# Bank readings ahead of the weights' steps in a decoder block on one core, with a mean and roots of norms in other operations

## The chip, the core and the metric

The kernel is one launch on one core of a Trainium2 chip. TensorE (PE) multiplies and writes into banks of PSUM, VectorE (DVE) and ScalarE (ACT) read and empty these banks and do the elementwise work, GpSimd (POOL) and SyncE (SP) issue DMAs. Each engine works through its own list of instructions in order, and waits at an instruction until what it reads is written and what it writes is free. The metric is the time of one execution on the device in microseconds (us), as a median over runs.

## The reference

A hybrid decoder block, in f32, over 512 tokens of width 1024:

```python
h = h + 0.5 * swiglu(rms_norm(h, g_ffn1), w_ffn1_gate, w_ffn1_up, w_ffn1_down)   # inner width 2816
u = rms_norm(h, g_mix)
z = u @ w_in                          # conv GLU | q | k | v | merge gates
y_conv = conformer_conv(a_glu, ...)   # GLU, 31-tap depthwise conv, LayerNorm, silu, @ w_conv_out
y_attn = o.reshape(b, s, ATTN_OUT_W) @ w_attn_out      # dilated windowed attention, 3 groups
h = h + (g_a * y_conv + g_b * y_attn) @ w_mix_out      # the mixers' output
h = h + 0.5 * swiglu(rms_norm(h, g_ffn2), w_ffn2_gate, w_ffn2_up, w_ffn2_down)
gate = sigmoid(rms_norm(h, g_ple) @ w_ple_gate)
h = h + gate * (p @ w_ple_proj)       # the embedding
return rms_norm(h, g_final)
```

`rms_norm` multiplies by the inverse root of the mean of squares plus 1e-6; the LayerNorm after the convolution also subtracts the mean over the 1024 channels.

## The kernel before

An f32 product is made of three products of rounded numbers (`float32r`): both operands are split into a high part and a remainder, and high x high, remainder x high and high x remainder are summed in one bank (`mm3`, L474 to L476). Weights come from HBM in slabs of 128 x 1024 numbers, which live in one pool of sixteen places ("w"). The names are `wr` for a slab as loaded (or a sum of slabs), `s` for a sum, `wh` for the high part, `wl` for the remainder. The remainder is made in one of two ways: by DVE (`wl = r - wh`, L403, behind ACT's copy L402), or by DMA: ACT writes the negated high part into `wl` (L372), and POOL issues a DMA that adds the loaded slab to it (L374).

The two FFNs and the mixers' output save products by Winograd's form of two-by-two blocks: seven products instead of eight ("by sevens"). The seven of a unit are named B11, B21, T2, T1, T3, B22, T4; `PRODUCTS` gives their order in an FFN and `MIXED` in the mixers. Several of the seven are summed in the same PSUM bank one after the other:

```python
BANKS = {"B11": "pa", "B21": "pe", "T2": "pa", "T1": "pd", "T3": "pa", "B22": "pd", "T4": "pa"}
```

so B11, T2, T3 and T4 share pa. Between two of them that bank must be read: ACT copies it (L956) or DVE adds it to what was collected (L969 in an FFN, L776 in the mixers). The next product into the bank waits for that reading. Each unit also needs sums of weight blocks (L340 to L353 in an FFN, L317 to L325 and L340 in the mixers), sums of inputs (`t`, L681) and their two parts (`bh`/`b`, `bl`, L693 and L696). These last are kept in a list `later` and spread over the steps by `QUOTA` (FFN) and `AFTER_M` (mixers).

What sets the order on the engines is the order in which the code is written. Each step calls `slab(key)`, which is `take` (hand over the weights prepared earlier) and `advance` (prepare later ones):

```python
def slab(key):
    z = take(key)
    advance()
    return z
```

`advance` calls `prepare`, which works some units ahead: it issues loads on SP, sums of weights on DVE, and the splits of weights on ACT, DVE and POOL. All of that stands in the engines' queues where `advance` is called, so ahead of the reading of the bank that the step ends with.

An FFN begins with two pairs of output blocks by plain quarters (`EARLY = 2`, weights "gq"), since the norm's factor `R` is not there yet; the next pair, `j == EARLY`, is the first by sevens (`gate_up`). FFN 1 comes at the start of the span; FFN 2 begins right behind the mixers. The mixers' loop runs over two halves `g` and the seven products, with four adds into `h` per pair of banks (DVE, `gx<-gx,p`, L776; `gx` is the memory in which `h` lies). At the end comes the embedding: `pp`, the product of `p` with `w_ple_proj`, in two halves of four banks (L1693 to L1695, emptied by ACT, L1697); sixteen transposes (L788) of `h`, made by `over`, stand between the first two banks and the last two of the first half, and give the inputs of the gate `pg`, whose weights are split by L411 and L412 (`pgh`, `wl`).

The convolution's mean is one f32 product of the channel sum `csum` with a constant matrix of 1/1024 (`average`, L1557), at step 3 of a list `lns` that runs beside the gates' products. The inverse roots of the norms are made by `rsqrt` on numbers per token (128 x 4), from the bits of the argument and three Newton steps: eleven DVE operations. `by_token` calls it five times, four times of `Rows` (norms over `h`) and once of `Norm` (the convolution's). Then, where the norm is spread over a bank, `diag` and PE's products with `one_r` follow (`spread`).

Of the kernel before, what the change touches and what calls it, by code (L numbers as in the profile page):

```python
# [152 lines left out]
def block_kernel(ctx: ExitStack, tc: tile.TileContext, a, out):  # L153
# [359 lines left out]
    one_r = const.tile([P, P], F32R, name="one_r")  # L513
    warm = const.tile([P, 1], F32, name="warm")
    V.memset(one, 1.0)
    V.memset(mean, 1.0 / D)
    V.tensor_copy(one_r, one)
    A.activation(warm, mean[:, 0:1], AF.Silu)
# [53 lines left out]
    def rsqrt(m, y, t):  # L572
        V.tensor_scalar(t.bitcast(I32), m.bitcast(I32), 1, None, op0=OP.logical_shift_right)
        V.tensor_scalar(y.bitcast(I32), t.bitcast(I32), -1.0, MAGIC, op0=OP.mult, op1=OP.add)
        for _ in range(3):
            V.tensor_mul(t, m, y)
            V.scalar_tensor_tensor(t, t, -0.5, y, op0=OP.mult, op1=OP.mult)
            V.scalar_tensor_tensor(y, t, 1.5, y, op0=OP.add, op1=OP.mult)

    class Norm:  # L580
# [18 lines left out]
        def total(self, m):  # L599
# [9 lines left out]
            V.tensor_scalar(m, p[:, :NB], EPS, None, op0=OP.add)  # L609

        def by_token(self, diag=True):
            m, y, t = (small.tile([P, NB], F32, name=name(q), tag="nt" + q, bufs=2) for q in "myt")
            self.total(m)
            rsqrt(m, y, t)
# [23 lines left out]
    class Rows(Norm):  # L638
# [10 lines left out]
        def total(self, m):  # L649
            V.scalar_tensor_tensor(m, self.cols[:, :NB], EPS, self.cols[:, NB:], op0=OP.add, op1=OP.add)  # L650

# [143 lines left out]
    def ffn(n, xs, u, norm, out_, soon_=None, last_=None):  # L795
# [142 lines left out]
        def gate_up(j):  # L938
# [6 lines left out]

            for q in PRODUCTS:
                wh, wl = slab((n, ("gu", j), q))
# [19 lines left out]
                else:  # L967
                    z = t[{"B21": "B11", "T3": "T1", "B22": "T2"}[q]]
                    V.tensor_add(z, z, p)  # L969
                    spend(0, 0.69)  # L970
                    if q != "T3":
                        zs = z.rearrange("p (c s) -> p c s", s=256)
                        r_ = both_halves(lo if q == "B21" else hi)
                        job(lambda zs=zs, r_=r_: V.tensor_mul(zs, zs, r_), 0, 0.69)
# [8 lines left out]
                for _ in range(min(QUOTA.get(q, 0) + 2 * (q == "T3" and j == KF // 2 - 2), len(later))):  # L983
                    next_job(later)
# [570 lines left out]
    def average():  # L1555
        lead["mean"] = p = bank("pm")
        PE.matmul(p, mean, summed[0], start=True, stop=True)  # L1557
# [14 lines left out]
    lns = [nothing, nothing, nothing, average] + [lambda i=i: center((i, i + 1)) for i in range(0, KD, 2)]  # L1572
# [72 lines left out]
    for g in range(2):  # L1645
        ps = banks()
        for q in MIXED:
            wh, wl = slab(("m", ("mx", g), q))
# [6 lines left out]
            add(q, p)  # L1655
            if g and q == "T4":
                over(xs, V_G2, mid, us2)
# [186 lines left out]
```

## Time and profile before

| | us |
|---|---|
| median of 3 runs | 1270.28 (1270.25 to 1270.64) |
| the profiled execution | 1270.42 |
| its span, first to last instruction | 1268.7 |
| DVE rows L403 (89 remainders of weights) | 108.7 |
| ACT rows L372 (92 copies of `wr` for remainders by DMA) | 96.7 |

A row of the timeline has the start and the duration in us, the engine, the line, the operation with output<-inputs, shapes, and how many; in brackets the idle time before it and what ended it. A row of waits has the engine and the line that waited, for what, then the sum in us, the times and the longest. A row of windows has the window, its length, then for PE, PEld, DVE, ACT and POOL the busy us with the count, the granted clock of TensorE (1.00 is full speed), the busy share of the DMA engines and GB/s. The first line of the page has busy us, share of the span and count of each engine; the next shows the shares of the chain that ended last.

### The profile page before, as it was taken

How to read it: one execution, taken by the hardware profiler on the slowest of the kernel's cores; microseconds unless marked ns; L12 is line 12 of the kernel's file. 1: busy time of each engine (PE TensorE's matmuls, PEld its weight loads, DVE VectorE, ACT ScalarE, POOL GpSimd, SP SyncE). 2: the span in 40 equal slices, each digit the busy share in tenths (PEclk: the TensorE clock that was granted, in tenths of full speed). 3: DMA queues.
4: the chain of work that ended last, by engine and by line, in shares of the span. 5: the costliest groups of instructions: out<-in, count | busy, mean ns of one | idle time of the engine just before them, and what ended most of it. 6: DMA issues, size and time to landing. Idle time of an engine off the chain costs nothing.

```text
span 1268.7 us, 19687 instructions
## 1 busy us (share of the span) xinstructions
PE 1258.6 (99%) x7394; PEld 1117.5 (88%) x7394; DVE 1057.2 (83%) x1715; ACT 738.4 (58%) x1077; POOL 233.9 (18%) x305
## 2 busy tenths in 40 slices
PE   9999999999999999999999999999999999999997
PEld 7898999999888889889898888878898999999886
DVE  6988898988989988888888654697589988988975
ACT  7666666665643254747465545365475666665673
POOL 0011111110222232323332222125111111110100
PEclk9999999999999999999999999999999999999999
DMA  7378778776788798888888777759668778775631
GB/s 272 102 158 206 174 182 203 171 183 173 175 195 206 177 181 195 153 189 155 171 169 189 178 174 164 196 140 270 153 156 212 161 194 196 173 181 166 166 100 67
DMA packets 120982, 222.83 MB, mean 176 GB/s; under 512 B 19128, under 2 KB 63544, under 8 KB 120888
## 3 DMA queue, kind: packets, MB, share of 16 engines
q0 software_dynamic: 47440, 138.96, 53.7%
q1 hardware_dynamic: 73016, 82.10, 20.3%
q8 instruction: 58, 0.95, 0.3%
q10 hardware_dynamic: 432, 0.52, 0.1%
q14 instruction: 36, 0.29, 0.1%
HBM read 168.56 MB, written 2.13 MB: 135 GB/s over the span
## 4 chain that ended last, share of the span: by engine, by line
PE 76%; issue 11%; DVE 5%; ACT 3%; POOL 3%; DMA 1%; DVEq 0%; POOLq 0%; ACTq 0%
PE pa L752 5%; PE pa L753 5%; PE pa L755 5%; PE pq L474 4%; PE pq L476 4%; PE pq L475 4%; PE pa L767 3%; PE pa L762 3%; PE pa L763 3%; PE pd L753 2%; PE pd L755 2%; PE pd L752 2%; POOL wh L271 2%; PE pd L763 1%; PE pd L767 1%
## 5 line engine op out<-in xcount | busy, mean ns | idle before, releaser
L374 POOL DMA_DIRECT2D wl<-wr x92 | 79.7, 866 | 596.6 <-ACT wl L372 400.0
L1185 DVE SCALAR_TENSOR_TENSOR acc<-glu,taps,acc 128x511 f32<-128x511 f32 (+14 forms) x240 | 161.3, 734 | 0.0
L403 DVE TENSOR_TENSOR wl<-s,wh 128x1024 fp32r<-128x1024 f32 x89 | 108.7, 1221 | 29.8 <-ACT wh L402 29.8
L372 ACT ACTIVATE wl<-wh 128x1024 fp32r<-128x1024 f32 x84 | 87.8, 1051 | 66.2 <-DMA wh<-in_w_in 37.5
L402 ACT ACTIVATE wh<-s 128x1024 fp32r<-128x1024 f32 x89 | 93.2, 1051 | 38.0 <-PE pa L767 14.0
L372 ACT ACTIVATE wl<-wr 128x1024 fp32r<-128x1024 f32 x92 | 96.7, 1051 | 19.6 <-PE pd L767 9.9
L752 PE MATMUL pa<-bh,wh 128*128 128x256 f32 x432 | 106.2, 284 | 0.3 <-DVE p L969 0.3
L753 PE MATMUL pa<-bl,wh 128*128 128x256 f32 x432 | 106.0, 283 | 0.0
L386 ACT ACTIVATE wh<-wr 128x1024 fp32r<-128x1024 f32 x92 | 96.3, 1046 | 4.5 <-PE pe L763 4.5
L374 POOL DMA_DIRECT2D wl<-in_w_in x56 | 50.1, 896 | 224.4 <-ACT wl L372 220.1
L474 PE MATMUL pq<-xsh,wh 128*128 128x512 f32 x224 | 88.7, 396 | 0.0
L475 PE MATMUL pq<-xsl,wh 128*128 128x512 f32 x224 | 87.4, 390 | 0.0
L476 PE MATMUL pq<-xsh,wl 128*128 128x512 f32 x224 | 87.3, 390 | 0.0
L752 PEld LDWEIGHTS pa<-bh,wh 128*128 128x128 f32 x432 | 82.9, 192 | 0.9 <-DVE p L969 0.5
L753 PEld LDWEIGHTS pa<-bl,wh 128*128 128x128 f32 x432 | 83.0, 192 | 0.0
L474 PE MATMUL pg<-xsh,wh 128*128 128x512 f32 x192 | 76.7, 399 | 0.4 <-ACT wh L544 0.2
L475 PE MATMUL pg<-xsl,wh 128*128 128x512 f32 x192 | 75.1, 391 | 0.2 <-DVE xsl L503 0.2
L476 PE MATMUL pg<-xsh,wl 128*128 128x512 f32 x192 | 75.0, 391 | 0.0
L778 DVE SCALAR_TENSOR_TENSOR gx<-pa,half,gx 128x512 f32<-128x512 f32 x80 | 56.3, 746 | 8.9 <-PE pa L767 8.9
L755 PE MATMUL pa<-bh,wl 128*128 128x256 f32 x432 | 60.7, 283 | 0.0
L956 ACT ACTIVATE p<-pa 128x512 f32<-128x512 f32 x36 | 21.5, 597 | 66.5 <-PE pa L755 66.0
L755 PEld LDWEIGHTS pa<-bh,wl 128*128 128x128 f32 x432 | 55.7, 192 | 0.0
(371 smaller groups left out, 3847.4 us busy)
## 6 DMA issues: line engine op xcount, KB each, us to landing
wl<-wr POOLq DMA_DIRECT2D x92, 512.0 KB, 5.1
wh<-in_w_in POOLq DMA_DIRECT2D x56, 512.0 KB, 7.2
wl<-in_w_in POOLq DMA_DIRECT2D x56, 512.0 KB, 6.1
wr<-in_w_ffn_down SPq DMA_DIRECT2D x44, 512.0 KB, 5.3
wr<-in_w_ffn_up SPq DMA_DIRECT2D x80, 256.0 KB, 4.6
wr<-in_w_ffn_gate SPq DMA_DIRECT2D x78, 256.0 KB, 5.1
wh<-in_w_v POOLq DMA_DIRECT2D x16, 256.0 KB, 7.6
wl<-in_w_v POOLq DMA_DIRECT2D x16, 256.0 KB, 5.2
```

The lines of the kernel that those rows point to most:

```text
L372: A.activation(l.bitcast(F32R), h, AF.Copy, scale=-1.0)
L374: G.dma_start(to, src, accum_op=OP.add)
L386: A.activation(h, r, AF.Copy)
L402: A.activation(h, r, AF.Copy)
L403: V.tensor_sub(l, r, h.bitcast(F32))
L474: PE.matmul(ps, wh, xh, start=start, stop=False, skip_group_check=part)
L475: PE.matmul(ps, wh, xl, start=False, stop=False, skip_group_check=part)
L476: PE.matmul(ps, wl, xh, start=False, stop=stop, skip_group_check=part)
L752: PE.matmul(o, h[:, c], th, start=q in ("B11", "B21", "T1") and i == 0, stop=False, skip_group_check=True)
L753: PE.matmul(o, h[:, c], tl, start=False, stop=False, skip_group_check=True)
L755: PE.matmul(o, l[:, c], th, start=False, stop=i >= len(at) - 2, skip_group_check=True)
L1185: bg.append(lambda acc=acc, g=g, w=w, s=s: V.scalar_tensor_tensor(acc[:, s:], g[:, :S - s], w, acc[:, s:], op0=OP.mult, op1=OP.add))
```

## The change

Five edits:

- **First pair by sevens** (`gate_up`, `j == EARLY`, both FFNs): `take` and `advance` apart. For T3 of that pair `advance` is called after the bank's reading (L969) and not before the product; the pieces of `later` due after a step are written after the next step's `take` and `advance`; the scaling of B21's sum by `R` is written at once, not as a job.
- **Mixers**: `take` first, then the product, the readings (`add`), and only then `advance`.
- **Embedding**: for the first half `advance` comes after `over(gs, V_GP, high)` between the second and the third bank, for the second half directly after `take`.
- **Mean**: `csum` is split into a high part and a remainder, one step ahead of `average`; two products with a rounded matrix `mean_r` take the place of the f32 product. 1/1024 is a power of two.
- **Roots**: eight operations instead of eleven, on an argument scaled by `R_Z`; `Rows.total` has one operation more, `Norm.total` has the factor in an operation that it had. So each root of `Rows` has two operations fewer, that of `Norm` three.

```diff
--- before.py
+++ after.py
@@ -511,10 +511,12 @@
     one = const.tile([P, P], F32, name="one")
     mean = const.tile([P, P], F32, name="mean")
     one_r = const.tile([P, P], F32R, name="one_r")
+    mean_r = const.tile([P, P], F32R, name="mean_r")
     warm = const.tile([P, 1], F32, name="warm")
     V.memset(one, 1.0)
     V.memset(mean, 1.0 / D)
     V.tensor_copy(one_r, one)
+    V.tensor_copy(mean_r, mean)
     A.activation(warm, mean[:, 0:1], AF.Silu)
     p = bank("warm")
     for _ in range(N_WARM):
@@ -569,13 +571,15 @@
         halves[0], halves[1] = hl
         return x, xs, us
 
-    def rsqrt(m, y, t):
-        V.tensor_scalar(t.bitcast(I32), m.bitcast(I32), 1, None, op0=OP.logical_shift_right)
-        V.tensor_scalar(y.bitcast(I32), t.bitcast(I32), -1.0, MAGIC, op0=OP.mult, op1=OP.add)
-        for _ in range(3):
-            V.tensor_mul(t, m, y)
-            V.scalar_tensor_tensor(t, t, -0.5, y, op0=OP.mult, op1=OP.mult)
-            V.scalar_tensor_tensor(y, t, 1.5, y, op0=OP.add, op1=OP.mult)
+    def rsqrt(z, y, w, t):
+        V.tensor_scalar(y.bitcast(I32), z.bitcast(I32), -0.5, R_GUESS, op0=OP.mult, op1=OP.add)
+        V.tensor_mul(t, y, y)
+        V.tensor_mul(t, t, z)
+        V.scalar_tensor_tensor(t, t, R_A, t, op0=OP.add, op1=OP.mult)
+        V.scalar_tensor_tensor(w, t, R_B, y, op0=OP.add, op1=OP.mult)
+        V.tensor_mul(t, w, w)
+        V.tensor_mul(t, t, z)
+        V.scalar_tensor_tensor(y, t, R_C, w, op0=OP.add, op1=OP.mult)
 
     class Norm:
 
@@ -606,12 +610,12 @@
                 for i, t in enumerate(every):
                     PE.matmul(p[:, b:b + 1], t[:, b * P:(b + 1) * P], mean[:, 0:1], start=i == 0,
                               stop=i == len(every) - 1)
-            V.tensor_scalar(m, p[:, :NB], EPS, None, op0=OP.add)
+            V.tensor_scalar(m, p[:, :NB], EPS, R_Z, op0=OP.add, op1=OP.mult)
 
         def by_token(self, diag=True):
-            m, y, t = (small.tile([P, NB], F32, name=name(q), tag="nt" + q, bufs=2) for q in "myt")
+            m, y, w, t = (small.tile([P, NB], F32, name=name(q), tag="nt" + q, bufs=2) for q in "mywt")
             self.total(m)
-            rsqrt(m, y, t)
+            rsqrt(m, y, w, t)
             if diag:
                 yh, yl = (small.tile([P, NB], F32R, name=name(q), tag="nt" + q, bufs=2) for q in ("yh", "yl"))
                 V.tensor_copy(yh, y)
@@ -648,6 +652,7 @@
 
         def total(self, m):
             V.scalar_tensor_tensor(m, self.cols[:, :NB], EPS, self.cols[:, NB:], op0=OP.add, op1=OP.add)
+            V.tensor_scalar(m, m, R_Z, None, op0=OP.mult)
 
     jobs, later = [], []
 
@@ -943,8 +948,14 @@
                 form()
             both = us_.rearrange("p (c s) -> p c s", s=S)
 
+            quota, begins = 0, j == EARLY
             for q in PRODUCTS:
-                wh, wl = slab((n, ("gu", j), q))
+                wh, wl = take((n, ("gu", j), q))
+                if not (begins and q == "T3"):
+                    advance()
+                for _ in range(min(quota, len(later))):
+                    next_job(later)
+                quota = 0
                 if BANKS[q] not in ps:
                     ps[BANKS[q]] = bank(BANKS[q])
                 p = ps[BANKS[q]]
@@ -968,10 +979,15 @@
                     z = t[{"B21": "B11", "T3": "T1", "B22": "T2"}[q]]
                     V.tensor_add(z, z, p)
                     spend(0, 0.69)
+                    advance()
                     if q != "T3":
                         zs = z.rearrange("p (c s) -> p c s", s=256)
                         r_ = both_halves(lo if q == "B21" else hi)
-                        job(lambda zs=zs, r_=r_: V.tensor_mul(zs, zs, r_), 0, 0.69)
+                        if begins and q == "B21":
+                            V.tensor_mul(zs, zs, r_)
+                            spend(0, 0.69)
+                        else:
+                            job(lambda zs=zs, r_=r_: V.tensor_mul(zs, zs, r_), 0, 0.69)
                     if q == "B21":
                         job(lambda z=z: (A.activation(z, z, AF.Silu), t.update(gate=z)), 0.63)
                     elif q == "B22":
@@ -980,8 +996,11 @@
                             both[:, :, hi], t["T1"].rearrange("p (c s) -> p c s", s=256),
                             t["T2"].rearrange("p (c s) -> p c s", s=256))), 0, 0.69)
                 work(2.88)
-                for _ in range(min(QUOTA.get(q, 0) + 2 * (q == "T3" and j == KF // 2 - 2), len(later))):
-                    next_job(later)
+                quota = QUOTA.get(q, 0) + 2 * (q == "T3" and j == KF // 2 - 2)
+                if not begins:
+                    for _ in range(min(quota, len(later))):
+                        next_job(later)
+                    quota = 0
 
         ending = []
 
@@ -1553,8 +1572,10 @@
             cv.append(split(conv.pop(c), "cv"))
 
     def average():
+        h, l = lead.pop("sum")
         lead["mean"] = p = bank("pm")
-        PE.matmul(p, mean, summed[0], start=True, stop=True)
+        PE.matmul(p, mean_r, h, start=True, stop=False)
+        PE.matmul(p, mean_r, l, start=False, stop=True)
 
     def root():
         lead.pop("mean")
@@ -1569,7 +1590,7 @@
     def nothing():
         pass
 
-    lns = [nothing, nothing, nothing, average] + [lambda i=i: center((i, i + 1)) for i in range(0, KD, 2)]
+    lns = [nothing, nothing, lambda: lead.update(sum=split(summed[0], "csum")), average] + [lambda i=i: center((i, i + 1)) for i in range(0, KD, 2)]
     lns += [nothing, nothing, root, nothing, nothing, spread, lambda: normal((0, 1, 2, 3)),
             both(normal, (4, 5), swish, (0, 1)), both(normal, (6, 7), swish, (2, 3)),
             lambda: (lead.clear(), swish((4, 5))), lambda: swish((6, 7))]
@@ -1645,7 +1666,7 @@
     for g in range(2):
         ps = banks()
         for q in MIXED:
-            wh, wl = slab(("m", ("mx", g), q))
+            wh, wl = take(("m", ("mx", g), q))
             for z in mixes[2 * g:2 * g + 2]:
                 while q not in z:
                     next_job(later)
@@ -1653,6 +1674,7 @@
             rows_of(p, q, wh, wl, [z.pop(q) for z in mixes[2 * g:2 * g + 2]],
                     (lambda: over(xs, V_G2, low, us2)) if g and q == "T4" else None)
             add(q, p)
+            advance()
             if g and q == "T4":
                 over(xs, V_G2, mid, us2)
             for f in ending:
@@ -1680,10 +1702,13 @@
     pTh, pTl = slab(("pT",))
     pp = {}
     for j in range(2):
-        wh, wl = (z.rearrange("p (i k m) -> p k i m", i=4, k=2) for z in slab(("pp", j)))
+        wh, wl = (z.rearrange("p (i k m) -> p k i m", i=4, k=2) for z in take(("pp", j)))
+        if j:
+            advance()
         for b in range(NB):
             if j == 0 and b == 2:
                 over(gs, V_GP, high)
+                advance()
                 ending.pop()()
             if j and b == 3:
                 r = gnorm.by_token(diag=False)
```

The lists of SP and POOL have the same order as before. PE's list differs only at the mean. The other lists differ in the places named above; three of them, with the rows of before and then of the change.

DVE in FFN 1, from the sum L340 that stands in the queue while T2 and T3 run, to the reading of bank pd (B22). `wr` and `s` are weights, `tu` and `t` the inputs' sums, `p<-p,pa` the reading of the bank. Before:

```order
L403 TENSOR_TENSOR wl_762<-s_138_639,wh_761 128x1024
L340 TENSOR_TENSOR s_161_765<-wr_641,wr_644 128x1024
L681 TENSOR_TENSOR t_794<-tu_627,tu_626 128x256
L681 TENSOR_TENSOR t_794<-tu_627,t_682 128x256
L696 TENSOR_TENSOR bl_726<-t_682,bh_725 128x512
L344 TENSOR_TENSOR s_167_803<-s_161_765,wr_647 128x1024
L969 TENSOR_TENSOR p_792<-p_792,pa_650 128x512
L696 TENSOR_TENSOR bl_831<-t_794,bh_830 128x512
L348 TENSOR_TENSOR wr_641<-wr_647,wr_641 128x1024
L969 TENSOR_TENSOR p_756<-p_756,pd_767 128x512
```

Now (the reading has line L980, `t` L686, `bl` L701):

```order
L403 TENSOR_TENSOR wl_762<-s_139_640,wh_761 128x1024
L340 TENSOR_TENSOR s_162_765<-wr_642,wr_645 128x1024
L701 TENSOR_TENSOR bl_693<-tu_628,bh_692 128x512
L686 TENSOR_TENSOR t_795<-tu_628,tu_627 128x256
L686 TENSOR_TENSOR t_795<-tu_628,t_695 128x256
L701 TENSOR_TENSOR bl_731<-t_695,bh_730 128x512
L980 TENSOR_TENSOR p_793<-p_793,pa_651 128x512
L344 TENSOR_TENSOR s_168_829<-s_162_765,wr_648 128x1024
L348 TENSOR_TENSOR wr_642<-wr_648,wr_642 128x1024
L701 TENSOR_TENSOR bl_838<-t_795,bh_837 128x512
L980 TENSOR_TENSOR p_757<-p_757,pd_768 128x512
```

The reading of pa stood behind L344 and stands ahead of it now, directly behind the second remainder `bl`; another `bl` has moved from ahead of `wl` to behind L340.

DVE in the mixers, around the end of the first half (`pe` is B21's bank, `pa` T4's and then the next half's first). Before:

```order
L696 TENSOR_TENSOR bl_8353<-t_8332,bh_8352 128x512
L321 TENSOR_TENSOR s_1311_8377<-wr_8285,s_1310_8360 128x1024
L776 TENSOR_TENSOR gx<-gx,pe_8259 128x512
L776 TENSOR_TENSOR gx<-gx,pe_8260 128x512
L403 TENSOR_TENSOR wl_8394<-s_1305_8335,wh_8393 128x1024
L325 TENSOR_TENSOR wr_8209<-wr_8213,wr_8209 128x1024
L776 TENSOR_TENSOR gx<-gx,pa_8257 128x512
L776 TENSOR_TENSOR gx<-gx,pa_8258 128x512
L403 TENSOR_TENSOR wl_8419<-s_1310_8360,wh_8418 128x1024
L776 TENSOR_TENSOR gx<-gx,pa_8412 128x512
L776 TENSOR_TENSOR gx<-gx,pa_8413 128x512
```

Now (`add` has line L781):

```order
L701 TENSOR_TENSOR bl_8356<-t_8335,bh_8355 128x512
L781 TENSOR_TENSOR gx<-gx,pe_8262 128x512
L781 TENSOR_TENSOR gx<-gx,pe_8263 128x512
L321 TENSOR_TENSOR s_1316_8394<-wr_8302,s_1315_8377 128x1024
L781 TENSOR_TENSOR gx<-gx,pa_8260 128x512
L781 TENSOR_TENSOR gx<-gx,pa_8261 128x512
L403 TENSOR_TENSOR wl_8411<-s_1310_8352,wh_8410 128x1024
L325 TENSOR_TENSOR wr_8212<-wr_8216,wr_8212 128x1024
L781 TENSOR_TENSOR gx<-gx,pa_8415 128x512
L781 TENSOR_TENSOR gx<-gx,pa_8416 128x512
L403 TENSOR_TENSOR wl_8436<-s_1315_8377,wh_8435 128x1024
```

The pair of `pe` has moved ahead of L321, the pair of `pa` ahead of the remainder L403 and of L325, and these two now stand between that pair and the next half's first.

ACT in the embedding, from the split of `pp`'s second weight to the copies of transposed tiles (`xsh<-tp`). Before:

```order
L423 ACTIVATE wh_12262<-wr_12154 128x1024
L411 ACTIVATE pgh_12273<-wr_12170 128x512
L411 ACTIVATE pgh_12276<-wr_12170 128x512
L1697 ACTIVATE pp_12288<-pp_12281 128x512
L1697 ACTIVATE pp_12297<-pp_12290 128x512
L494 ACTIVATE xsh_12304<-tp_12299,gx 128x512
L494 ACTIVATE xsh_12313<-tp_12308,gx 128x512
```

Now (L1722 is the copy of pp):

```order
L423 ACTIVATE wh_12264<-wr_12156 128x1024
L1722 ACTIVATE pp_12281<-pp_12274 128x512
L1722 ACTIVATE pp_12290<-pp_12283 128x512
L494 ACTIVATE xsh_12297<-tp_12292,gx 128x512
L494 ACTIVATE xsh_12306<-tp_12301,gx 128x512
L494 ACTIVATE xsh_12315<-tp_12310,gx 128x512
L494 ACTIVATE xsh_12324<-tp_12319,gx 128x512
L411 ACTIVATE pgh_12329<-wr_12172 128x512
L411 ACTIVATE pgh_12332<-wr_12172 128x512
```

The two `pgh` rows have moved behind two copies of `pp` and four copies of transposed tiles.

## Prediction

> **What bounds the kernel now.** I read the page's busy times first, then the chain that ended last, then the list of what PE waited for, and only then the rows of each place that the diff touches.
>
> ```profile
> PE 1258.6 (99%) x7394; PEld 1117.5 (88%) x7394; DVE 1057.2 (83%) x1715; ACT 738.4 (58%) x1077; POOL 233.9 (18%) x305
> PE 76%; issue 11%; DVE 5%; ACT 3%; POOL 3%; DMA 1%; DVEq 0%; POOLq 0%; ACTq 0%
> core 0: 1268.7 us, clock 0.998
> PE pa L752 <- DVE p L969: 0.3, 1, 0.3
> PE pa L762 <- DVE gx L776: 0.2, 1, 0.2
> ```
>
> TensorE (PE) is busy 99% of the span at a granted clock of 0.998: nothing that VectorE (DVE) or ScalarE (ACT) saves counts unless PE waits for it, and the change leaves PE's list of work as it is except for one product. So the sum is over PE's waits, and those on record are small: the last two rows are two of six. The list understates them, because ends of matmuls are modelled; I measure a wait from starts, as the distance between equal steps.
>
> **Change part by part.** The profiled execution took 1270.42 us, 1.7 more than its span and 0.14 more than the median, 1270.28. I sum against 1270.42 and take 0.14 off at the end.
>
> *First pair by sevens (`gate_up`, `j == EARLY`).* PE's rows at the last product T4 of FFN 1:
>
> ```profile
> 68.56 1.12 PE L755 MATMUL pa<-bh,wl 128*128 128x256 f32 x8
> 71.44 1.12 PE L755 MATMUL pd<-xsh,wl 128*128 128x256 f32 x8
> 72.86 0.39 PE L752 MATMUL pa<-bh,wh 128*128 128x256 f32 x1 [0.30 <-DVE p L969]
> 74.88 0.52 PE L755 MATMUL pa<-bh,wl 128*128 128x256 f32 x3
> 70.39 0.69 DVE L696 TENSOR_TENSOR bl<-t,bh 128x512 fp32r<-128x512 f32 x1
> 70.99 1.22 DVE L344 TENSOR_TENSOR s<-s,wr 128x1024 f32<-128x1024 f32 x1
> 72.12 0.68 DVE L969 TENSOR_TENSOR p<-p,pa 128x512 f32<-128x512 f32 x1
> ```
>
> A step is 71.44 - 68.56 = 2.88 us from the eight products by `wl` of one to those of the next; the step of T4 takes 74.88 - 71.44 = 3.44. T4 writes bank pa, and DVE reads T3 out of that bank (L969) only at 72.12, behind a remainder (L696) and a sum of the next weights (L344, 1.22). In the new order L969 stands ahead of L344, so it can start by 71.58 at the latest (where L344's place is, plus one L696 of 0.60) and probably before 71, since the weights' copies on ACT, for which DVE waits earlier, move forward too. T4 would start at 71.44 + 8 x 0.12 = 72.4, and the read would take 0.68: done between 71.6 and 72.3. Term: **-0.56**, between 0 and -0.56. What stood ahead of the read (L344) comes at most 0.7 us later than in the old order, and PE has no wait for a weight's sum here that this could lengthen. FFN 2 runs the same code, but I found no long step there, so its term is 0. The scaling of B21 by `R`, done at once, is the same instruction earlier.
>
> *Mixers.* The four products of L767 that end the first round of a step stand in PE's queue at 2.72 us in an undisturbed step (851.37 - 848.65):
>
> ```profile
> 843.08 1.07 PE L767 MATMUL pe<-wl,bh 128*128 128x512 f32 x4
> 845.93 1.07 PE L767 MATMUL pa<-wl,bh 128*128 128x512 f32 x4
> 848.65 0.62 PE L767 MATMUL pa<-wl,b 128*128 128x512 f32 x2
> 851.37 1.07 PE L767 MATMUL pd<-wl,b 128*128 128x512 f32 x4
> 852.66 0.47 PE L762 MATMUL pa<-wh,b 128*128 128x512 f32 x1 [0.22 <-DVE gx L776]
> 854.67 1.07 PE L767 MATMUL pa<-wl,b 128*128 128x512 f32 x4
> 848.36 1.23 DVE L325 TENSOR_TENSOR wr<-wr,wr 128x1024 f32<-128x1024 f32 x1
> 849.49 1.29 DVE L776 TENSOR_TENSOR gx<-gx,pa 128x512 f32<-128x512 f32 x2
> 850.69 1.23 DVE L403 TENSOR_TENSOR wl<-s,wh 128x1024 fp32r<-128x1024 f32 x1
> 851.82 1.29 DVE L776 TENSOR_TENSOR gx<-gx,pa 128x512 f32<-128x512 f32 x2
> ```
>
> T4 of the first half took 845.93 - 843.08 = 2.85, T2 of the second 854.67 - 851.37 = 3.30: excess 0.13 + 0.58 = 0.71 us. In both PE waits for a pair of additions (L776) that stands behind a step of the weights. With the additions first, I replay DVE with these durations (1.20 for a pair, 1.13 from one long operation to the next): the pair of T4 is done near 848.4, then L403 to 849.6, L325 to 850.7, and the pair of B11 at 850.7 to 851.9. T2 would begin at 852.66 - 0.58 - 0.13 = 851.95 on its first bank, free after one addition, at 851.3. Margin 0.6 on the first bank, about 0.1 on the second. Term: **-0.71**, bounds 0 and -0.71. But L325, the sum that becomes T3's weight, starts some 1.2 us later: see the rival on DMA.
>
> *Embedding.* PE transposes sixteen tiles (L788) and then needs a bank that ACT empties:
>
> ```profile
> 870.96 1.91 PE L788 MATMUL tp<-ident,gx 128*128 128x128 f32 x16
> 872.62 0.48 PE L474 MATMUL pg<-xsh,wh 128*128 128x512 f32 x1
> 1206.68 1.91 PE L788 MATMUL tp<-ident,gx 128*128 128x128 f32 x16
> 1208.71 0.50 PE L1693 MATMUL pp<-wh,wh 128*128 128x512 f32 x1
> 1207.04 1.14 ACT L411 ACTIVATE pgh<-wr 128x512 fp32r<-128x512 f32 x2
> 1208.07 1.08 ACT L1697 ACTIVATE pp<-pp 128x512 f32<-128x512 f32 x2
> ```
>
> The same sixteen take 872.62 - 870.96 = 1.66 in FFN 2 and 2.03 here. The copies of pp move ahead of the two pgh copies, to 1207.04, so the first is done by 1207.7, before 1206.68 + 1.66 = 1208.34. Term: **-0.37**. The pgh copies come some 3.5 us later (two copies of pp and four of transposed tiles ahead of them); the embedding's gate products that read them stand behind all products of pp in PE's order, so I give them no term; uncovered they would cost up to that.
>
> *Mean.* One f32 product becomes two rounded ones:
>
> ```profile
> 721.05 1.02 PE L1557 MATMUL pm<-csum,mean 128*128 128x512 f32 x2
> 721.51 0.79 PE L474 MATMUL pg<-xsh,wh 128*128 128x512 f32 x1
> 722.14 0.40 PE L475 MATMUL pg<-xsl,wh 128*128 128x512 f32 x1
> 722.38 0.39 PE L476 MATMUL pg<-xsh,wl 128*128 128x512 f32 x1
> 719.41 0.69 DVE L1596 TENSOR_TENSOR sg<-pg,R 128x512 f32<-128x512 f32 x1 [3.91 <-PE pg L476]
> 720.13 0.63 ACT L1597 ACTIVATE sg<-sg 128x512 f32<-128x512 f32 x1 [4.52 <-DVE sg L1596]
> ```
>
> From L1557 to L475 are 1.09 us, of which one rounded product (722.38 - 722.14 = 0.24, 0.23 elsewhere) is L474: the mean costs 0.86. Two rounded products cost 0.46. Term: **-0.40**. The split adds one copy on ACT and one subtraction on DVE (0.63 and 0.69 for this shape); both engines had been idle 4 us (the two last rows), so it is covered. Without that cover PE would wait for some 1.3 us.
>
> *Roots.* Five roots lose two or three operations on 128x4 each, such as:
>
> ```profile
> 745.03 0.16 DVE L578 SCALAR_TENSOR_TENSOR y<-t,y 128x4 f32<-128x4 f32 x1
> ```
>
> That is 11 x 0.16 = 1.8 us of busy DVE, but none of PE's waits is for a root's output, as it has products queued there: 0, at best 3 x 0.16 = -0.5 at the root of the convolution's norm, and -0.3 at each of the others, if one was waited for. The cast of `mean_r` runs while the start waits for DMA: 0.
>
> Gains: 0.56 + 0.71 + 0.37 + 0.40 = 2.04 us, 1268.38 on the profiled execution and **1268.2** on the median's basis.
>
> **Rivals.** *The first weights of FFN 2 come later (the part I expect).* Around the end of the mixers the software queue of DMA is full:
>
> ```profile
> 870.00:890.00 20.00, 20.00 (x98) 16.75 (x98) 15.92 (x48) 9.77 (x18) 7.52 (x10) 1.00 1.13 298
> 852.07 0.88 POOL L374 DMA_DIRECT2D wl<-wr  x1 [6.50 <-ACT wl L372]
> 876.49 1.78 POOL L374 DMA_DIRECT2D wl<-in_w_ffn_up  x2 [6.61 <-ACT wl L372]
> 886.63 0.88 POOL L374 DMA_DIRECT2D wl<-in_w_ffn_gate  x1 [0.79 <-DMA wl<-in_w_ffn_up]
> 887.47 0.39 PE L476 MATMUL pu<-xsh,wl 128*128 128x512 f32 x1
> ```
>
> The first row has the DMA share at 1.13 (engines full). The burst begins with POOL's accumulate of T3's remainder at 852.07, behind L372, behind L325. A remainder issued at 876.49 has landed by 886.63, and PE uses it at 887.47: 0.84 us to spare. If L325's 1.2 us pass through a full queue, and PE comes 0.71 earlier relative to it, PE waits 1.2 + 0.71 - 0.84 = 1.07 us. Against it: POOL itself waited 6.61 ahead of 876.49, so part can be caught up. Between 0 and 1.07 I take half, **+0.5**: 1268.2 + 0.5 = **1268.7**. The Trainium skill ("DMA: Bandwidth & Descriptors", section "Anatomy of one DMA — SWDGE (gpsimd) path") fits 2.0 us plus bytes / 436 GB/s for such a DMA, 2.6 us for 256 KB. By that rule the remainder would have 8 us to spare, nothing would be given back and the time would be 1268.2; the rows above show about 10 us from issue to landing, with the queue shared, so I don't follow it here.
>
> *All four waits go and nothing comes back:* 1268.2.
>
> *The waits only move.* The second bank at T2 has 0.1 us to spare, DVE is full there, and the reading at T4 of FFN 1 relies on ACT's copies. If the mixers' 0.71 and the 0.56 stay, the gain is 0.77: 1269.5, and with the 0.5 above 1270.0.
>
> *Slower: the burst's delay repeats.* POOL takes its queue in order; an accumulate waits for ACT's negated copy, which waits for the landing of the weight's first part. The two pairs by quarters take eight weights in this way; if five of them add another 1.2 us each instead of passing one delay on, PE loses 5 x 1.2 + 0.71 - 0.84 = 5.9 us and the time is 1268.2 + 5.9 = 1274.1. It decides from 4.6 us (1272.8 - 1268.2). POOL's waits of 6.61 and 0.79 speak against: they are slack of the issuer.
>
> **How the numbers follow.** 0.2%, 2.54 us, is about what a measurement of this kernel can tell from no change: faster is below 1267.74, slower above 1272.82. Chances: partial give-back 0.43 (1268.7), none 0.30 (1268.2, of which 0.06 is below 1267.74, if a root gives its 0.5), waits that move 0.15 (1269.5 to 1270.0), burst repeating 0.06 (1274.1), and 0.06 for a wait that no row shows, half of it on the faster side, a third on the slower. That makes faster 0.06 + 0.03 = 0.09, slower 0.06 + 0.02 = 0.08, same 0.83. The range goes from 1267.6, the full gain with a root's 0.5, to 1270.3, waits that move with the give-back, and 0.3 for the spread of the runs.
>
> **What would show it.** T4 of the first pair 2.88 us after T3; the L767 rows of the mixers all 2.72 apart; sixteen transposes in 1.66 at the embedding; 0.46 between the last L1439 and L474's regular place at the mean; and in FFN 2 a new wait of PE L476 for DMA near 887, of 0 to 1.1 us. I am wrong if PE waits for a weight's sum or copy in either first pair, or if a root was waited for.

## The result and the profile after

| | us |
|---|---|
| before, median of 22 runs | 1270.29 (1269.86 to 1271.73) |
| changed, median of 22 runs | 1268.53 (1268.04 to 1270.62) |
| ratio | 0.9986, 95% interval 0.998 to 0.9992 |
| profiled execution, before and changed | 1270.42 and 1268.50 |
| its span, before and changed | 1268.7 and 1266.7 |

The medians are 1.76 us apart, 0.14%: the same by the 0.2% of the prediction, which had 1268.7, though the interval of the ratio lies below 1, so a small gain is clear of the noise. The two profiled executions are 1.92 us apart. First the page of the changed kernel, busy times and chain, and then its list of PE's waits:

```profile
PE 1257.6 (99%) x7394; PEld 1117.9 (88%) x7394; DVE 1056.4 (83%) x1706; ACT 738.5 (58%) x1078; POOL 234.4 (19%) x305
PE 99%; DVE 0%; DMA 0%; ACT 0%; issue 0%; DVEq 0%; ACTq 0%
```

```profile
PE warm L523 <- DVE one L516: 1.1, 1, 1.1
PE pg L474 <- DVE xsh L502: 0.2, 1, 0.2
PE pg L475 <- DVE xsl L503: 0.2, 1, 0.2
```

The waits for `p` and for `gx` (0.3 and 0.2 before) are gone, and the chain that ended last is PE for 99% of the span, where it was 76%. Now PE's timeline of the changed kernel at the four places of the sum, in order of time (line numbers are shifted: L760 was L755, L772 was L767, L793 was L788, L1718 was L1693):

```profile
68.69 1.12 PE L760 MATMUL pa<-bh,wl 128*128 128x256 f32 x8
71.57 1.12 PE L760 MATMUL pd<-xsh,wl 128*128 128x256 f32 x8
74.45 1.12 PE L760 MATMUL pa<-bh,wl 128*128 128x256 f32 x8
...
720.63 0.39 PE L1577 MATMUL pm<-csumh,mean_r 128*128 128x512 f32 x1
720.86 0.39 PE L1578 MATMUL pm<-csuml,mean_r 128*128 128x512 f32 x1
721.09 0.39 PE L474 MATMUL pg<-xsh,wh 128*128 128x512 f32 x1
...
842.24 1.07 PE L772 MATMUL pe<-wl,bh 128*128 128x512 f32 x4
844.96 1.07 PE L772 MATMUL pa<-wl,bh 128*128 128x512 f32 x4
847.68 0.84 PE L772 MATMUL pa<-wl,b 128*128 128x512 f32 x3
850.40 1.07 PE L772 MATMUL pd<-wl,b 128*128 128x512 f32 x4
853.12 0.61 PE L772 MATMUL pa<-wl,b 128*128 128x512 f32 x2
...
1205.13 1.91 PE L793 MATMUL tp<-ident,gx 128*128 128x128 f32 x16
1206.80 0.48 PE L1718 MATMUL pp<-wh,wh 128*128 128x512 f32 x1
```

T4 of the first pair takes 74.45 - 71.57 = 2.88 us (3.44 before); the mixers' T4 and T2 take 2.72 each (2.85 and 3.30); the sixteen transposes 1206.80 - 1205.13 = 1.67 (2.03); the mean 721.09 - 720.63 = 0.46 (0.86). That is 0.56 + 0.71 + 0.36 + 0.40 = 2.03 us. The start took 68.69 - 68.56 = 0.13 more in this execution, so 1.90 are to be seen at the end, and 1.92 are.

DVE of the changed kernel in the first pair, and ACT in the embedding:

```profile
70.34 0.68 DVE L980 TENSOR_TENSOR p<-p,pa 128x512 f32<-128x512 f32 x1
70.94 1.22 DVE L344 TENSOR_TENSOR s<-s,wr 128x1024 f32<-128x1024 f32 x1
```

```profile
1205.49 1.07 ACT L1722 ACTIVATE pp<-pp 128x512 f32<-128x512 f32 x2
```

The reading of pa starts at 70.34, not 72.12, and is over by 71.02, 1.5 us before T4 begins at 72.5; the copies of pp end at 1206.56, ahead of the transposes' end.

### The profile page after: what moved, and what is told of

It reads as the page before. It is cut to its first block, busy times and chain, and to the rows that moved or that the text cites. A ratio compares the mean times of both kernels' runs of the same rounds, so it can differ in the third digit from the quotient of the medians.

```text
span 1266.7 us, 19688 instructions
## 1 busy us (share of the span) xinstructions
PE 1257.6 (99%) x7394; PEld 1117.9 (88%) x7394; DVE 1056.4 (83%) x1706; ACT 738.5 (58%) x1078; POOL 234.4 (19%) x305
## 3 DMA queue, kind: packets, MB, share of 16 engines
q1 hardware_dynamic: 73016, 82.10, 20.3%
## 4 chain that ended last, share of the span: by engine, by line
PE 99%; DVE 0%; DMA 0%; ACT 0%; issue 0%; DVEq 0%; ACTq 0%
PE pa L757 5%; PE pa L760 5%; PE pa L758 5%; PE pq L474 4%; PE pq L475 4%; PE pq L476 4%; PE pa L767 3%; PE pg L475 3%; PE pa L768 3%; PE pa L772 3%; PE pg L474 3%; PE pg L476 3%; PE pd L758 3%; PE pd L757 3%; PE pd L760 3%; PE pb L474 2%
## 5 line engine op out<-in xcount | busy, mean ns | idle before, releaser
L403 DVE TENSOR_TENSOR wl<-s,wh 128x1024 fp32r<-128x1024 f32 x89 | 108.6, 1220 | 29.9 <-ACT wh L402 29.9
L372 ACT ACTIVATE wl<-wh 128x1024 fp32r<-128x1024 f32 x84 | 87.8, 1051 | 69.6 <-DMA wh<-in_w_in 37.7
L372 ACT ACTIVATE wl<-wr 128x1024 fp32r<-128x1024 f32 x92 | 96.7, 1051 | 19.1 <-PE pd L772 9.9
L476 PE MATMUL pq<-xsh,wl 128*128 128x512 f32 x224 | 87.3, 390 | 0.0
L476 PE MATMUL pg<-xsh,wl 128*128 128x512 f32 x192 | 74.9, 390 | 0.0
L760 PE MATMUL pa<-bh,wl 128*128 128x256 f32 x432 | 60.6, 283 | 0.0
L760 PEld LDWEIGHTS pa<-bh,wl 128*128 128x128 f32 x432 | 55.7, 192 | 0.0
```

The source lines that it names most:

```text
L372: A.activation(l.bitcast(F32R), h, AF.Copy, scale=-1.0)
L403: V.tensor_sub(l, r, h.bitcast(F32))
L476: PE.matmul(ps, wl, xh, start=False, stop=stop, skip_group_check=part)
L760: PE.matmul(o, l[:, c], th, start=False, stop=i >= len(at) - 2, skip_group_check=True)
```

## The experiments

My theory (A in the expectations): each edit removes one wait of PE, the parts add up, and the mixers' edit alone puts something at risk, the first weights of FFN 2. The rivals: the parts are given back later (B), the spread of the times comes from elsewhere (C, D), and, formed after the second group of runs, F: that time is lost at the embedding's gate.

All times below are medians of 11 runs, taken in three groups; the kernel before ran 33 times beside each group and had 1270.30, 1270.60 and 1270.74. An interval of 11 runs is some 0.0009 wide to each side, 1.1 us, so terms of 0.4 are read from the profiles; the medians only bound them. "Gate" below is the time from the first product of the embedding's gate that reads `pgh` to the start of the last product of the kernel.

**One edit at a time, put into the kernel before.** Each kernel has the hunks of the front's diff for one edit alone. First `gate_up`:

> The kernel before with the edit of gate_up alone. Theory A (each edit removes one wait of PE, the parts add up, and the mixers' edit alone makes the first weights of FFN 2 tight): T4 of FFN 1's first pair starts 2.88 us after T3's place instead of 3.44, 0.56 less, median near 1269.7, runs as close together as those of before (0.5 us for most). Rival B (all the edits together are needed, since PE's gain in FFN 1 is only waited for later): the 0.56 is gone from the profile by the middle of the span, median within 0.2 of 1270.3.

Measured 1270.37 (1269.42 to 1271.8; ratio 0.9997, 0.9988 to 1.0006). PE's timeline of this kernel, first pair and then the mixers:

```profile
71.91 1.12 PE L755 MATMUL pd<-xsh,wl 128*128 128x256 f32 x8
74.79 1.12 PE L755 MATMUL pa<-bh,wl 128*128 128x256 f32 x8
```

```profile
832.01 1.07 PE L767 MATMUL pd<-wl,b 128*128 128x512 f32 x4
835.14 1.07 PE L767 MATMUL pa<-wl,b 128*128 128x512 f32 x4
```

The step is 2.88 us, so the wait is removed, but the median doesn't show it: a miss of my expected 1269.7. In the profiled execution the start took about 0.46 more, and the mixers, whose order is the old one here, 0.6 more than before's: their third step took 835.14 - 832.01 = 3.13 us, 0.41 of it new. A had not allowed for either. The late third step doesn't come from the mixers' order: the last run below shows it in the new order as well, and the traces read there show what it goes with. B isn't borne out: nothing ties that step to `gate_up`, and `e3_emb` below, whose edit lies behind the mixers, shows it too.

Then the mixers alone:

> The kernel before with the mixers' edit alone. Theory A: the products of L767 are all 2.72 us apart, 0.73 us less at the end of the mixers; in FFN 2 the remainder that lands last ahead of the second half of pair 0 has about 0.1 to 0.5 us to spare instead of 1.1, so some executions lose up to 1 us again: median 1269.6 to 1270.0, and runs spread over 1 to 2 us upward. Rival C (the spread of the changed kernel's times comes from elsewhere): median 1269.5 and runs within 0.5 us of each other.

Measured 1269.83 (1269.10 to 1270.97; ratio 0.9994, 0.9986 to 1.0003). All steps of L767 are 2.72 us. From the first product by sevens of the mixers to FFN 2's first product its profile has 39.76 us, as the changed kernel's has, and before 40.50: 0.74 less. The median lies in A's range, but the kernel before spread over 2.5 us in the same group, so that separates nothing. FFN 2 shows no wait of PE for the remainder, though only 0.04 us were to spare there: its second half landed at 885.97, and PE's weight load, which works ahead of PE, took it at 886.01.

The embedding and the mean alone:

> The kernel before with the embedding's edit alone. Theory A: the sixteen transposes take 1.66 us to the next product instead of 2.03, median 1269.9, runs as close together as before. Rival C2 (the later pgh copies make the gate's products wait for weights in some executions): the profile shows a wait of PE for pgh or wl near 1217 to 1230, and the runs spread upward.

Measured 1270.23 (ratio 0.9999, 0.999 to 1.0007). The transposes take 1.66 us and the gate 43.71, as long as before's, so the later `pgh` copies made nothing wait. The mixers, again in the old order, took 41.24 us, 0.74 more than before's 40.50, of which 0.51 is again the third step; this hides the gain.

> The kernel before with the mean by two rounded products alone (csum split one step earlier). Theory A: 0.40 us less between the last product of the attention and the gates' next product, nothing waits for csum, median 1269.9. Rival: the step before average is too late for the split, PE waits for ACT or DVE there by 0.3 us or more, median 1270.2 or above.

Measured 1269.91 (ratio 0.9996, 0.9988 to 1.0005). The 0.40 us are gone at the mean and nothing waits for `csum`.

> The kernel before with the shorter roots alone (8 operations for 11). Theory A: nine to eleven DVE operations of 0.16 us fewer, but PE waits for no root, so the median is within 0.2 us of the kernel before and no row of PE's starts moves by more than 0.1 us at the roots. Rival: a root is waited for somewhere, 0.3 us or more less in total.

Measured 1270.63 beside 1270.60 (ratio 1.0002, 0.9993 to 1.001). No start of PE moves by over 0.1 us at a root: the eleven operations fewer (DVE has 1704 instructions in this kernel, 1715 before) are worth nothing here. The changed kernel has nine fewer, since the mean's edit adds two.

**Two edits taken out of the changed kernel.**

> The changed kernel without the mixers' edit. Theory A: 0.73 us of the profile's gain is back (the mixers' steps of 2.85 and 3.30 us), about 1.33 us remain; no execution loses anything in FFN 2, so the median is 1268.9 to 1269.0 with most runs within 0.5 us. Rival C (the spread comes from elsewhere): the runs spread as the changed kernel's do, over more than 1 us.

Measured 1269.47 (1268.75 to 1271.68; ratio 0.9993, 0.9984 to 1.0002), against 1268.53 and 1268.52 for the two sets of runs of the changed kernel: about 1.0 us, with intervals that overlap. The profile agrees: 40.83 us for the mixers, 39.76 with the edit, and 0.13 of the difference is the third step. But the runs spread without the mixers' edit too, which speaks against A and for C. This profile shows where, in the waits of PEld, in SP's queue (`row` and `gf` are the final norm's gains) and in PE's first and last product of the gate:

```profile
PEld pg L1733 <- DVE wl L412: 1.1, 4, 0.4
PEld pg L1731 <- ACT pgh L411: 0.4, 1, 0.4
```

```profile
1195.18 0.83 SPq L1696 DMA_DIRECT2D row<-in_gx  x1
1209.46 0.82 SPq L1699 DMA_DIRECT2D gf<-row  x2
1210.39 7.49 SPq L271 DMA_DIRECT2D wr<-in_w_ple_gate  x5
```

```profile
1215.63 0.39 PE L1731 MATMUL pg<-pgh,xsh 128*128 128x512 f32 x1
1260.17 0.28 PE L1733 MATMUL pg<-wl,xsh 128*128 128x256 f32 x1
```

SP issues `row`, then waits 1209.46 - 1195.18 - 0.83 = 13.45 us until it has landed, and the last five weights of the gate stand behind. PE comes to the gate at 1215.63, and the gate takes 44.54 us, 0.83 more than in an execution without a wait. I took this as theory F for the last group of runs.

> The changed kernel without the embedding's edit. Theory F: the 0.37 us at the transposes come back in the profile, but part of them is waited for at the gate anyway, so the median rises by 0 to 0.3 us. Rival G: it rises by the whole 0.37.

Measured 1269.24 beside 1268.52 for the changed kernel in the same group: 0.72 more, at least the whole 0.37 of G, though the intervals of the two overlap. Its profile has the 0.37 at the transposes and 43.72 at the gate. F's claim that part of this edit's gain is given back at the gate isn't borne out.

**A late remainder in FFN 2.** The place where I had expected 0.5 us to be given back, with its issue delayed (shortened):

```diff
         A.activation(l.bitcast(F32R), h, AF.Copy, scale=-1.0)
+        if late:                 # order[i] == ("gq", "2", 0, 3)
+            G.tensor_copy(l.bitcast(F32R), l.bitcast(F32))
```

> The changed kernel with one copy of 128x1024 on POOL (in place, no change of the numbers) between ACT's negated copy and the issue of the remainder of the fourth weight of FFN 2's first pair: the issue is later by what the trace shows for the copy, x us, estimated at 1 to 2. Theory A (that remainder has 0.1 to 0.5 us to spare): PE waits x - 0.1 to x - 0.5 us at L476 near 885, and the median rises by about as much. Rival D (there are microseconds to spare, the spread is something else): no wait, median within 0.2 us of the changed kernel's.

Measured 1268.42 (ratio 0.9984, 0.9975 to 0.9992). POOL of this kernel, then the same issue in the changed kernel:

```profile
874.76 1.54 POOL L374 CAST wl<-wl 128x1024 fp32r<-128x1024 f32 x1 [4.16 <-ACT wl L372]
876.61 1.78 POOL L376 DMA_DIRECT2D wl<-in_w_ffn_up  x2 [0.30 <-POOL wl L374]
```

```profile
874.94 1.78 POOL L374 DMA_DIRECT2D wl<-in_w_ffn_up  x2 [4.47 <-ACT wl L372]
```

Each row stands for two DMAs of 256 KB, one for each half of the remainder. The first half goes into the products of bank pg, the second into those of pu, so PE's L476 of bank pu waits for the second. The time from issue to landing of the two (least and most) is, first in the changed kernel and then in this one:

```profile
DMA to landing us min/median/max: 9.5/9.8/10.2
```

```profile
DMA to landing us min/median/max: 7.9/8.3/8.7
```

The second half was issued at 875.50 and landed 10.2 us later, at 885.74, in the changed kernel; here it was issued at 877.16 and landed 8.7 us later, at 885.84. PE's load of that weight, and PE's product, in the changed kernel and then here:

```profile
885.78 0.19 PEld L476 LDWEIGHTS pu<-xsh,wl 128*128 128x128 f32 x1
```

```profile
885.92 0.40 PE L476 MATMUL pu<-xsh,wl 128*128 128x512 f32 x1
```

```profile
885.88 0.19 PEld L478 LDWEIGHTS pu<-xsh,wl 128*128 128x128 f32 x1 [0.16 <-DMA wl<-in_w_ffn_up]
```

The issue is 876.61 - 874.94 = 1.67 us later, but the landing only 0.10. The weight load waited 0.16 us, and PE, which it works ahead of, lost nothing. In the changed kernel the load began 885.78 - 885.74 = 0.04 us behind the landing; in the kernel before it was 887.24 - 886.34 = 0.90, near my 0.84. So D has the outcome, no wait and the same median, but not its reason: there were no microseconds to spare. A was about right on the margin and wrong in letting the delay of the issue reach the landing. In this stretch, with the DMA engines' share at 1.13 (the prediction's row, before), the time of the issue didn't set the time of the landing. That the transfers ahead of it did, on engines that were full, is likely and not shown.

**The same remainder made by DVE** from a load on SP's queue (shortened):

```diff
-  ... or key[:2] == ("gq", "2"))
+  ... or key[:2] == ("gq", "2") and key != ("gq", "2", 0, 3))
```

> The changed kernel with that fourth weight's remainder made by ACT and DVE from a load on SP's queue, not by the software queue: 0.5 MB of accumulation less in the full stretch, one load, one copy and one subtraction more elsewhere. Theory A: the tight landing is gone, the runs come together, median 1268.2 (all of 2.07 us kept) unless the load or DVE's subtraction is late in its turn. Rival C: median and spread as the changed kernel's, 1268.5 with runs over 1 us apart. Rival E: the subtraction comes late behind DVE's other work and PE waits for it, median above 1268.6.

Measured 1271.13 (1269.94 to 1274.31; ratio 1.0008, 0.9999 to 1.0017), 2.6 us worse than the changed kernel. PE's waits:

```profile
PE pg L474 <- DVE xsh L502: 0.4, 1, 0.4
PE pu L476 <- DMA wl<-in_w_ffn_gate: 0.3, 1, 0.3
PE pg L475 <- DMA wl<-in_w_ffn_gate: 0.2, 1, 0.2
```

None of the three outcomes as written: the median is E's, but the subtraction wasn't late. A had excepted a load that comes late in its turn, and what came late here are other transfers. SP has two more loads, of half a megabyte together, at 854.88 and 855.28, and the first part of FFN 2's first gate weight landed at 863.81, against 862.34 in the changed kernel. ACT's negated copy waited for it:

```profile
863.92 1.06 ACT L372 ACTIVATE wl<-wh 128x1024 fp32r<-128x1024 f32 x1 [4.76 <-DMA wh<-in_w_ffn_gate]
```

That copy starts 1.47 us later than in the changed kernel (862.45), and ACT's copies of PE's transposes stand behind it, so PE waits for `xsh`; the weight's remainder came late too, 869.51 instead of 867.40. Counted from the start of the mixers, PE is about 1.7 us behind the changed kernel at 868. So this stretch is near its limit of DMA after all: the delayed issue was covered, an added transfer was not.

**The row's DMA early.** `row` issued ahead of the mixers' preparation, in both kernels (shortened):

```diff
+    row = dram.tile([1, D], F32, name="row")
+    nc.sync.dma_start(row..., in_gx...)
     mixes, begun = [{} for _ in range(4)], []
...
-    row, gf = dram.tile([1, D], F32, name="row"), [T("gf") for _ in range(2)]
-    nc.sync.dma_start(row..., in_gx...)
+    gf = [T("gf") for _ in range(2)]
```

> The changed kernel with the DMA of the final norm's gains (row, 1024 numbers of 4 bytes) issued ahead of the mixers and not in the embedding, so that SP no longer waits about 13 us for it with the gate's last five weights behind. Theory F (what single executions give back is lost at the embedding's gate, where PE waits for weights that stand on SP's queue behind that DMA): SP issues the five loads some 10 us earlier, no PE or PEld wait for pgh or wl of the gate, runs closer together, median 0.1 to 0.5 us below the changed kernel's of the same call. Rival G (the spread is the start's and the mixers', the row's wait is covered): median within 0.1 us of the changed kernel's, same spread.

> The kernel before with that DMA issued early. Theory F: PE of the kernel before comes later at the gate and waits for less there, so the gain is smaller: 0 to 0.4 us. Rival G: within 0.1 us.

Measured 1272.89 (ratio 1.0021, 1.0012 to 1.003) and 1275.13 (1.0029, 1.002 to 1.0039). Each is 4.4 us slower than the kernel it was put into, beside it in the same group (1268.52 and 1270.74), which neither F nor G had. SP's queue and PE's waits in the second, then the gate of the first (SP's five loads, PE's first and last product):

```profile
681.87 2.06 SPq L1266 DMA_DIRECT2D other<-st  x4
683.97 0.81 SPq L1626 DMA_DIRECT2D row<-in_gx  x1
```

```profile
PE po L474 <- ACT pt L1418: 1.1, 1, 1.1
```

```profile
1201.13 10.30 SPq L271 DMA_DIRECT2D wr<-in_w_ple_gate  x5
```

```profile
1219.26 0.39 PE L1733 MATMUL pg<-pgh,xsh 128*128 128x512 f32 x1
1262.97 0.28 PE L1735 MATMUL pg<-wl,xsh 128*128 128x256 f32 x1
```

At the gate F is right: the loads are issued from 1201.13 and the gate takes 43.71 us, no wait. But SP had nothing else to do after the attention's last exchange (`other<-st`), and so `row`, 1024 numbers of 4 bytes, went out right behind that exchange at 683.97. What the exchange brings is first read by DVE, here in the kernel before and then with `row` early:

```profile
691.50 0.17 DVE L1384 TENSOR_TENSOR jm<-own,other 128x8 f32<-128x8 f32 x1 [1.68 <-DMA other<-st]
```

```profile
696.12 0.17 DVE L1384 TENSOR_TENSOR jm<-own,other 128x8 f32<-128x8 f32 x1 [6.65 <-DMA other<-st]
```

The exchange's last DMA landed 12.6 us after its issue here, 13.7 us in the changed kernel with `row` early, and 7.7 us in both kernels without. The attention's `pt` came later, and PE waited for it (1.1 us here, 1.9 in the other; in the kernel before, PE didn't wait there). In the changed kernel with `row` early the granted clock was also 0.50 for 3.4 us from 713.95, behind that wait; at half speed that is an estimated 1.7 us more; in the kernel before with `row` early it stayed at 1.00. Only `row`'s place differs, so the later landing comes from it; that it is the row's small packets that hold up the exchange isn't shown. Issuing `row` at a quieter place, between 690 and 780 say, wasn't tried.

**The changed kernel again:**

> The changed kernel itself, for comparison on the same chip. Theory F: median 1268.4 to 1268.6; where its profile shows a wait at the gate, the row's DMA took more than about 13.3 us, where it shows none, less. Rival G: waits at the gate have nothing to do with that DMA's time.

Measured 1268.52 beside 1270.74 (ratio 0.9984, 0.9975 to 0.9992). In this execution `row` took 14.05 us, and the gate 43.98: a wait of 0.27, both as F had it. Its mixers have the late third step, though the order is the new one (PE's timeline, then its waits):

```profile
831.14 1.07 PE L772 MATMUL pd<-wl,b 128*128 128x512 f32 x4
834.76 1.07 PE L772 MATMUL pa<-wl,b 128*128 128x512 f32 x4
```

```profile
PE pa L767 <- ACT wh L402: 0.6, 1, 0.6
```

The third step took 3.62 us, 0.90 too long, as PE waited for ACT's copy of T2's weight. I followed that copy back through ACT's and DVE's rows: each starts when the other hands over its input, and the chain begins at ACT's copy of the last weight of the convolution's output, which waits for its load. In the first execution of the changed kernel and then in this one:

```profile
806.17 1.06 ACT L372 ACTIVATE wl<-wh 128x1024 fp32r<-128x1024 f32 x1 [3.12 <-DMA wh<-in_w_conv_out]
```

```profile
807.34 1.06 ACT L372 ACTIVATE wl<-wh 128x1024 fp32r<-128x1024 f32 x1 [3.01 <-DMA wh<-in_w_conv_out]
```

All profiled executions but the two with `row` early, in us, by how long before the mixers' first product that load landed ("mixers to FFN 2" is from the mixers' first product to FFN 2's first):

| kernel | order of the mixers | load landed before | third step | mixers to FFN 2 |
|---|---|---|---|---|
| mixers alone | new | 21.11 | 2.72 | 39.76 |
| mean alone | old | 20.87 | 2.72 | 40.48 |
| changed, no embedding | new | 20.83 | 2.72 | 39.77 |
| changed | new | 20.76 | 2.72 | 39.76 |
| before | old | 20.54 | 2.72 | 40.50 |
| changed, remainder by DVE | new | 20.44 | 2.72 | 40.36 |
| changed, no mixers | old | 20.18 | 2.85 | 40.83 |
| changed, late remainder | new | 20.01 | 3.00 | 40.07 |
| roots alone | old | 19.94 | 3.06 | 41.08 |
| first pair alone | old | 19.88 | 3.13 | 41.16 |
| embedding alone | old | 19.78 | 3.23 | 41.24 |
| changed, again | new | 19.37 | 3.62 | 40.67 |

Below about 20.3 the third step grows by as much as the load is late, in both orders. Without that growth the new order takes 39.8 us (but for the remainder by DVE, which lost time elsewhere), and the old one 40.5, or 40.7 to 40.75 where the third step is late: the edit of the mixers is worth 0.7 to 1.0. No experiment moved this load, and why its landing varies is open.

The gate of the same executions, in the order of the last column but one. "Lead" is the time from the issue of `gf` to PE's first product of the gate; "second load" is how long after that product the second of the five loads behind `row` landed:

| kernel | wait for `row` | lead | second load | gate |
|---|---|---|---|---|
| before | 12.80 | 7.23 | 3.21 | 43.71 |
| mixers alone | 12.47 | 7.55 | 3.56 | 43.72 |
| changed, no embedding | 12.70 | 7.33 | 3.58 | 43.72 |
| embedding alone | 12.46 | 7.12 | 3.65 | 43.71 |
| changed | 13.17 | 6.44 | 4.00 | 43.71 |
| first pair alone | 13.38 | 6.64 | 4.12 | 43.78 |
| changed, late remainder | 13.77 | 5.84 | 4.24 | 43.90 |
| changed, again | 14.05 | 5.57 | 4.33 | 43.98 |
| changed, remainder by DVE | 14.68 | 4.94 | 4.40 | 44.09 |
| mean alone | 13.84 | 6.19 | 4.46 | 44.08 |
| roots alone | 13.96 | 6.05 | 4.69 | 44.26 |
| changed, no mixers | 13.45 | 6.17 | 4.97 | 44.54 |

With a lead of 6.4 us and more the gate takes 43.7 to 43.8 us; with less, 43.9 to 44.5. The loss does not grow evenly with the missing lead, but it does with the landing of the second load: beyond some 4.05 us, each further one costs 0.9 to 1.1. That goes with F, whose point that these loads stand behind `row` the two kernels with `row` early show by experiment. How long the loads themselves take varies too, and why is open.

## Why the prediction was right, point by point

- **First pair, -0.56**: measured 3.44 to 2.88 us, -0.56. The reading was over 1.5 us before it was needed, since ACT's copies moved forward as assumed. FFN 2 gained nothing there, as forecast.
- **Mixers, -0.71**: measured -0.71 at the two steps (-0.74 over the stage). The cause, additions behind a step of the weights, is as I had it. Where the third step is late the old order cost 0.94 to 0.99 and not 0.74, so the size comes from one kind of execution. The third step's own delay of 0.1 to 0.9 us stands in no term of the sum, and the change doesn't remove it.
- **Embedding, -0.37**: -0.36. **Mean, -0.40**: -0.40. **Roots, 0**: 0 within what can be read.
- **Give-back in FFN 2, +0.5: the step that failed.** I let the 1.2 us by which L325 comes later run through the full queue to the remainder's landing, and took half of the 1.07 us of wait that this made. At the start of the burst the delay is there: T3's accumulate is issued at 852.45, not 852.07, while PE was 0.81 us ahead at the mixers' start, so 1.19 later against PE. At the landing of the half that PE waits for, little of it is left: 885.74, not 886.34, so 0.20 later against PE in the same count. With the 0.90 to spare before and PE's 0.74 gained in the mixers, that leaves about nothing, measured 0.04, and no wait of PE: 0 given back and not 0.5. The issue of that remainder moved with PE (876.49 to 874.94, PE's use 887.47 to 885.92), since POOL is released there by ACT's L372, which stands behind copies of PE's transposes; but the copy that delayed it by 1.67 us shows that this isn't what sets the landing. What does is open. The rule for such a DMA (the Trainium skill, "DMA: Bandwidth & Descriptors", section "Anatomy of one DMA — SWDGE (gpsimd) path") gives an estimate of 2.6 us for 256 KB. By it nothing would be given back, which is what came, but not for its reason: the profile has 9.5 and 10.2 us for the two halves, and not 8 us to spare but 0.04.
- **The time itself, 1268.7 against 1268.53**: that it is so near is luck. Without the 0.5 that failed, my sum was 1268.2, and 2.03 off this median of before is 1268.26. Single executions lose up to 0.8 at the gate when `row` is late, and up to 0.9 at the mixers' third step, none of which the sum had. Whether these make the 0.27 between 1268.26 and 1268.53 isn't shown, since one profile per kernel says nothing of how often they occur, and the start varies by some tenths. Nor is it shown that anything is missing: the interval of the ratio goes from 1.0 to 2.5 us, which holds 2.03.

## What to carry to other kernels

Where one engine bounds the kernel, measure its waits as the distance between equal steps: lists of waits showed 0.5 us of the 1.3 us that two edits took away. Before letting a delay run through a queue of DMA, compare landings and not issues: here an issue 1.67 us later landed 0.10 later. Where one issue stands for several DMAs, take the landing of the one that the waiting engine reads. And a transfer that is moved early lands in another stretch: look at what stands beside it there, too; here an exchange landed 5 us later for it.

## What I had not expected of the hardware

SP stood 12.5 to 14.7 us behind one DMA of 1024 numbers of 4 bytes each, 4 KB in all, before it could issue the one that reads it, and that spread of 2 us goes with a wait of PE at the gate in half of these twelve executions. Issued behind the attention's exchange of small rows, the same DMA made the kernel 4.4 us slower.

In FFN 2's first pair a remainder of 256 KB landed at nearly the same time, 885.74 and 885.84, whether it was issued at 875.50 or at 877.16. And in one execution with `row` early, where PE had stood for 1.9 us, the granted clock was at half for 3.4 us right after; in another, behind 1.1 us, it was not.
